# Twelve idle matrix products at the start, and position biases loaded as one run per query, in a two-layer diffusion backbone

## The chip, the cores and the metric

The kernel runs on one core of one Trainium2 chip. The metric is the device time of one execution in microseconds (us); lower is better. The engines are TensorE (PE in the profile, its weight loads PEld), VectorE (DVE), ScalarE (ACT), GpSimd (POOL) and SyncE (SP, which here only issues transfers).

## The reference: what is computed

Two layers work on 256 latent tokens (a grid of 4 rows by 64 columns, 2048 channels each) and 256 context tokens, all in float32. Both layers begin with an adaptive normalisation whose scale, shift and gate come from a conditioning vector (adaln). The first layer holds 16 heads of neighbourhood attention and 32 state-space (SSD) heads side by side, between one input projection (14,400 columns) and one output projection; the second is a gated short convolution between two projections. What matters here is the start and the attention's bias:

```python
def adaln(cond, w, b):
    m = jax.nn.silu(cond) @ w + b
    return jnp.split(m, 3, axis=-1)
...
dr_idx = rs + jnp.arange(kh) - r + NA_KH - 1
bias = rpb[:, dr_idx[None, :, None], dc_idx[:, None, :]].reshape(nh, GRID_W, kh * GRID_W)
s_lat = jnp.einsum('bqhd,bkhd->bhqk', qr, kb).astype(jnp.float32) * scale + bias.astype(jnp.float32)
s_lat = jnp.where(mask, s_lat, -jnp.inf)
```

With four grid rows each query sees all four rows of keys. Its bias in a head depends only on the difference of the rows and of the columns: for query column c, key row a and key column k it is one element of the head's table of 15 by 31, at row (a - r + 7) and column (k - c + 15). Columns outside a window of 16 are masked.

## The kernel before: tiling, stages and order

**Precision.** A product of two float32 operands is made of three passes of the fast float32r form: each operand is split into a high part (a cast, on ScalarE) and a low part (the difference, on VectorE). A weight block of 128 x 1024 is loaded into one of the `raw` buffers by SP (line 428), cast into `wH` (line 458), and its low part goes into `wL` (line 465). Only when the low part is done is the raw buffer free for the next load.

**Start.** The conditioning vector becomes `csil` and is spread into `cpad`, a zero tile of 128 x 512 with two columns filled in every 32 (lines 548 to 556, the tile Btm). SP issues the two x tiles first, four blocks of 256 KB each (`x_load`, line 618), then the ada weights of 512 KB a block, then the first weights of the input projection. The x tiles are squared, summed and scaled in place (`x_norm`, lines 636 to 650), turned by 32 transposes on TensorE (`x_pair`, line 235 by the helper `turn`) and copied out of PSUM (lines 663 and 664). The scale and shift of the first 256 channels come from eight ada blocks (`ada_gen`): four 32-column products run side by side (line 231 by the helper `mm`), ScalarE copies the sum out (line 768), two transposes turn it, and VectorE adds. Then the normalised activations are made (`hH` and `hL`, lines 798 and 804) and the projection begins. In eight rounds of j this repeats for the next 256 channels, beside products for K, V, Q and B.

**Attention bias.** After the eight rounds the table is written once to `dram_rpbs`, each head's 320 relevant elements repeated for 64 query columns (line 967). In `head_gen`, a head loads its bias tile `bt` (128 partitions: two query rows of 64 columns each, by 3 x 256) with four transfers (line 1080), one for each grid row r of queries. In `dram_rpbs` the partitions step by 319 elements in rows of 320, so that each query starts one element further to the left, and four pieces of 64 elements (one per key row, 31 apart) are fetched per partition: 256 pieces of 256 bytes per transfer. VectorE adds the column mask (line 1085), and the maximum pass adds the bias to the scores (line 1098), once with the tile's first and last third (the last is zero, for the context keys), once with its second and last. Two tiles, bias0 and bias1, alternate; the loads of a head wait until the head two before it is done.

**Order.** The code is written as generators that a planner (`Plan`) interleaves: it keeps an estimated time for each engine and for the DMA, and emits a step when its inputs are expected. The order on every engine is fixed when the program is built. SP issues its transfers strictly in order, so a load whose buffer is free stands behind every transfer issued before it. In the program's rows every SP transfer also carries one of eight completion counters in turn.

**In the state-space part** (`dt_gen`, lines 1180 to 1260) a row of 128 values is broadcast to 128 partitions from the input `in_rows` (line 1184), and lines 1201 and 1203 on VectorE use it. This stands just behind the first two heads' bias loads in SP's order.

## Time and profile before

| What | Value |
|---|---|
| Runs | 1771.32, 1767.39, 1771.30 us; median 1771.3 |
| Profiled execution | 1762.67 us |
| Its span in the profile | 1760.9 us |
| Mean granted TensorE clock | 0.999 |
| VectorE, ScalarE busy | 73%, 45% |
| DMA | 412.5 MB, mean 234 GB/s |
| DMA packets | 147,629, of which 34,304 under 512 bytes |

The profile is of one execution. A row of a timeline reads: start and length in us, engine, line of the code, operation, output and inputs by the program's names with the buffer numbers left out, shapes, number; and in brackets how long the engine was idle before and what ended that. A row of a group ends with busy time in us and the mean of one in ns. In a row of windows, the busy time of PE, PEld, DVE, ACT and POOL (with counts) is followed by the granted clock, the share of time that the DMA engines were busy, and GB/s. A float32 product that is not of the float32r form shows as two records. A releaser is inferred: where the engine named had been done long before, a transfer was meant.

### The profile page before, as it was taken

Reading aid. Unit: us, or ns where it says so; the run is one execution under the profiler, and the core shown is the slowest. Engines: PE = TensorE matmul, PEld = TensorE weight load, DVE = VectorE, ACT = ScalarE, POOL = GpSimd, SP = SyncE. Lnnn points to the kernel's source line nnn. Section 1 sums busy time; section 2 is a strip of 40 time slices with the busy share of each in tenths; the row PEclk is TensorE's granted clock in tenths of the full one; section 3 lists DMA queues with packets and bytes.
Section 4 is the critical chain, followed back from the end, with each engine's and each line's share of the span. In section 5 each row is a group of like instructions: output and inputs, shape, how many; then the busy total and the mean of one; then the engine's idle time right before and its main releaser. Section 6 shows DMA issues by size and latency. Waiting matters only on the chain.

```text
span 1760.9 us, 25272 instructions
## 1 busy us (share of the span) xinstructions
PE 1728.3 (98%) x9305; PEld 1442.4 (82%) x9305; DVE 1292.8 (73%) x2041; ACT 785.3 (45%) x1186; POOL 191.0 (11%) x300
## 2 busy tenths in 40 slices
PE   6999999999999999999999999999999999999998
PEld 4677988889888889888888898888878888888887
DVE  5566877888787987786888698876667776766555
ACT  5422335454354453353453444654435444444442
POOL 0000111013111012111012101110000000000000
PEclk9999999999999999999999999999999999999999
DMA  9987675577876677866577767787766888876774
GB/s 349 344 291 252 214 227 181 181 214 241 261 227 201 190 219 248 262 193 204 170 239 227 215 188 226 224 261 253 268 216 232 265 281 266 267 248 216 219 231 158
DMA packets 147629, 412.50 MB, mean 234 GB/s; under 512 B 34304, under 2 KB 48272, under 8 KB 147504
## 3 DMA queue, kind: packets, MB, share of 16 engines
q1 hardware_dynamic: 132112, 366.64, 64.0%
q0 software_dynamic: 15392, 44.24, 8.0%
q8 instruction: 73, 1.20, 0.3%
q14 instruction: 52, 0.43, 0.1%
HBM read 386.53 MB, written 25.59 MB: 234 GB/s over the span
## 4 chain that ended last, share of the span: by engine, by line
PE 94%; DVE 2%; DMA 1%; ACT 1%; issue 1%; SPq 0%; POOL 0%; DVEq 0%; ACTq 0%; POOLq 0%
PE bank L231 93%; PE bank L235 1%; DVE wL L465 1%; DMA raw<-in_ada_w 0%; ACT wH L458 0%; DMA half<-in_rows 0%; DVE hL L804 0%; SPq L618 0%; DMA raw<-in_sc_in 0%; DVE tmp L1283 0%; DVE h L1729 0%; DVE tmp L800 0%; ACT h L1748 0%; ACT hH L798 0%; DVE xm L664 0%
## 5 line engine op out<-in xcount | busy, mean ns | idle before, releaser
L458 ACT CAST wH<-raw 128x1024 fp32r<-128x1024 f32 (+1 forms) x440 | 459.5, 1045 | 664.0 <-PE bank L231 559.6
L465 DVE TENSOR_TENSOR wL<-raw,wH 128x1024 fp32r<-128x1024 f32 (+1 forms) x440 | 532.2, 1213 | 257.4 <-ACT wH L458 255.0
L231 PE MATMUL bank<-hH,wH 128*128 128x256 f32 (+1 forms) x1040 | 341.0, 328 | 0.9 <-ACT wH L458 0.9
L231 PE MATMUL bank<-hL,wH 128*128 128x256 f32 (+1 forms) x1040 | 337.0, 324 | 0.0
L231 PE MATMUL bank<-hH,wL 128*128 128x256 f32 (+1 forms) x1024 | 331.4, 324 | 3.1 <-DVE wL L465 3.1
L231 PE MATMUL bank<-wH,h 128*128 128x512 f32 x1024 | 316.8, 390 | 1.7 <-DVE h L1729 1.7
L231 PE MATMUL bank<-wH,hH 128*128 128x512 f32 x640 | 256.0, 400 | 4.8 <-ACT hH L798 2.6
L231 PE MATMUL bank<-wL,hH 128*128 128x512 f32 x640 | 249.9, 391 | 0.3 <-DVE wL L465 0.3
L231 PE MATMUL bank<-wH,hL 128*128 128x512 f32 x640 | 249.3, 390 | 0.1
L231 PEld LDWEIGHTS bank<-wH,h 128*128 128x128 f32 x1024 | 191.9, 188 | 43.5 <-DVE h L1729 3.0
L231 PEld LDWEIGHTS bank<-hH,wH 128*128 128x128 f32 x1040 | 197.8, 190 | 18.9 <-issue 2.0
L231 PEld LDWEIGHTS bank<-hL,wH 128*128 128x128 f32 x1040 | 197.8, 190 | 15.8
L231 PEld LDWEIGHTS bank<-hH,wL 128*128 128x128 f32 x1024 | 194.6, 190 | 19.4 <-DVE wL L465 4.1
L857 DVE SCALAR_TENSOR_TENSOR acc<-raw,csil,acc 128x512 f32<-128x512 f32 x240 | 179.1, 746 | 30.9 <-DMA raw<-in_ada_w 27.2
L231 PE MATMUL bank<-wL,h 128*128 128x512 f32 x512 | 199.4, 389 | 0.2 <-DVE wL L465 0.2
L231 PE MATMUL bank<-wH,mix 128*128 128x512 f32 x512 | 160.9, 391 | 0.0
L231 PEld LDWEIGHTS bank<-wH,hH 128*128 128x128 f32 x640 | 120.1, 188 | 36.3 <-issue 7.2
L231 PEld LDWEIGHTS bank<-wH,hL 128*128 128x128 f32 x640 | 120.1, 188 | 25.4 <-DVE hL L804 0.6
L231 PEld LDWEIGHTS bank<-wL,hH 128*128 128x128 f32 x640 | 120.1, 188 | 25.0 <-DVE wL L465 1.1
L231 PEld LDWEIGHTS bank<-wL,h 128*128 128x128 f32 x512 | 96.1, 188 | 20.6 <-DVE wL L465 0.6
L231 PEld LDWEIGHTS bank<-wH,mix 128*128 128x128 f32 x512 | 96.1, 188 | 20.4 <-issue 0.5
L231 PE MATMUL bank<-wL,mix 128*128 128x512 f32 x256 | 99.7, 390 | 0.0
(276 smaller groups left out, 1856.5 us busy)
## 6 DMA issues: line engine op xcount, KB each, us to landing
raw<-in_w_in SPq DMA_DIRECT2D x209, 512.0 KB
raw<-in_ada_w SPq DMA_DIRECT2D x163, 512.0 KB
raw<-in_sc_in SPq DMA_DIRECT2D x128, 512.0 KB
raw<-in_w_out SPq DMA_DIRECT2D x64, 512.0 KB
raw<-in_sc_out SPq DMA_DIRECT2D x32, 512.0 KB
dram_ptd<-tmp POOLq DMA_DIRECT2D x32, 256.0 KB, 4.9
D<-dram_ptd POOLq DMA_DIRECT2D x64, 128.0 KB, 5.6
tmp<-dram_csr SPq DMA_DIRECT2D x32, 256.0 KB
```

Of the source, the lines that this page charges most:

```text
L231: E(T.matmul(o, l, r, start=start, stop=stop, skip_group_check=True))
L235: E(T.transpose(o, i, ident if k == 128 else ident[:k, :k]))
L458: E(S.copy(H, v))
L465: E(V.tensor_tensor(out=Lo, in0=v, in1=H.bitcast(F32), op=ALU.subtract))
L857: E(V.scalar_tensor_tensor(out=acc, in0=v[:, j], scalar=csil[:, 2 * k + j:2 * k + j + 1], in1=acc, op0=ALU.mult, op1=ALU.add))
```

## The change

**Idle products.** Right after the loads of the two x tiles are issued, 12 products of 128 x 256 are written for TensorE, into PSUM bank 7, whose content nobody reads before it is written again. Eight take both operands from `cpad`; four take the moving operand from the four blocks of the second x tile, so they wait for its loads. They go around the planner, which knows nothing of them.

**Bias.** The four pieces of a query lie 31 elements apart and are 64 long, so they overlap, and two query rows differ by 31 more. Each head now loads one contiguous run of 219 elements (876 bytes) per partition with two transfers, one per half of the partitions, to the end of the tile's first two thirds (`runs`, from column 293). The mask addition reads the overlapping pieces out of the run and writes them apart, from the front, into the same tile. The two halves of the tile have changed places, so line 1098 takes them the other way round. The planner is told to count each of the two transfers as two of the old kind.

```diff
+            twice = n == 4 * 64 * 219
             self.t[e] = s + (1200 if e == "POOL" else 450)
+            if twice:
+                n = 65536
+                self.dma = max(self.dma, s + 1000) + n / self.RATE
+                s += 450
+                self.t[e] += 450
...
     x_load(0)
     x_load(1)
+    flat = cpad.rearrange("p a b -> p (a b)")
+    for k in range(12):
+        T.matmul(free_b[7][:, :256], flat[:, :128], flat[:, :256] if k < 8 else XS[k - 4][:, :256], start=True, stop=True,
+                 skip_group_check=True)
     issue()
...
         yield W_("SP")
-        for r in range(4):
-            E(DMA.dma_start(bt[64 * (r % 2):64 * (r % 2) + 64, r // 2, :].rearrange("p (a b) -> p a b", a=4),
-                            bass.AP(tensor=b0.tensor, offset=b0.offset + hd * 64 * 320 + (7 - r) * 31 - 61,
-                                    ap=[[319, 64], [31, 4], [1, 64]])))
+        runs = bt[:, 0:2, :].rearrange("p q c -> p (q c)")[:, 293:]
+        for e in range(2):
+            E(DMA.dma_start(runs[64 * e:64 * e + 64],
+                            bass.AP(tensor=b0.tensor, offset=b0.offset + hd * 64 * 320 + 94 - 31 * e, ap=[[319, 64], [1, 219]])))
         yield W_("DVE", bt)
-        bv = bt[:, 0:2, :].rearrange("p q (r c) -> p (q r) c", c=64)
-        E(V.tensor_tensor(out=bv, in0=bv, in1=mask.unsqueeze(1).to_broadcast([128, 8, 64]), op=ALU.add))
+        E(V.tensor_tensor(out=bt[:, 0:2, :].rearrange("p q (r c) -> p q r c", c=64),
+                          in0=bass.AP(tensor=runs.tensor, offset=runs.offset, ap=[list(runs.ap[0]), [62, 2], [31, 4], [1, 64]]),
+                          in1=mask.unsqueeze(1).unsqueeze(1).to_broadcast([128, 2, 4, 64]), op=ALU.add))
...
-            E(V.tensor_tensor_reduce(out=two(sp), in0=two(ps), in1=bt[:, 1:3, :] if qt else bt[:, 0::2, :], scale=1.0,
+            E(V.tensor_tensor_reduce(out=two(sp), in0=two(ps), in1=bt[:, 0::2, :] if qt else bt[:, 1:3, :], scale=1.0,
```

The new lines push the rest of the code down by 6 to 11 lines, so line 231 of before is line 237 of the changed kernel, line 428 is 434 and line 1080 is 1091. The rows of the program below carry their own kernel's numbers.

TensorE at the very start of the program, before (raw are ada blocks, xs the x tiles, const the identity for the transposes):

```order
L2000 UNCONDITIONAL_BRANCH
L231 MATMUL bank_127<-raw_135,cpad 32x256 x4
L231 MATMUL bank_127<-raw_136,cpad 32x256 x4
L235 MATMUL bank_128<-const,xs_169 128x128
L235 MATMUL bank_128<-const,xs_177 128x128
```

And in the changed kernel:

```order
L2011 UNCONDITIONAL_BRANCH
L631 MATMUL bank_134<-cpad 128x256 x8
L631 MATMUL bank_134<-xs_177,cpad 128x256
L631 MATMUL bank_134<-xs_179,cpad 128x256
L631 MATMUL bank_134<-xs_181,cpad 128x256
L631 MATMUL bank_134<-xs_183,cpad 128x256
L237 MATMUL bank_127<-raw_135,cpad 32x256 x4
L237 MATMUL bank_127<-raw_136,cpad 32x256 x4
L241 MATMUL bank_128<-const,xs_169 128x128
L241 MATMUL bank_128<-const,xs_177 128x128
```

The twelve stand ahead of everything else; xs_177 to xs_183 are the second x tile. All rows behind them are the same as before, in the same order, and so are all rows of VectorE, ScalarE and GpSimd.

SP around the first two heads' bias loads, before (in_w_in and in_ada_w are weights):

```order
L428 DMA raw_135<-in_w_in 128x1024
L428 DMA raw_137<-in_w_in 128x1024
L1080 DMA bias_217<-dram_rpbs 64x4x64 x4
L1080 DMA bias_218<-dram_rpbs 64x4x64 x4
L428 DMA raw_139<-in_w_in 128x1024
L428 DMA raw_135<-in_w_in 128x1024
L428 DMA raw_136<-in_ada_w 128x1024
L428 DMA raw_138<-in_ada_w 128x1024
L428 DMA raw_137<-in_w_in 128x1024
L1184 DMA half_125<-in_rows 128x128
```

And in the changed kernel:

```order
L434 DMA raw_135<-in_w_in 128x1024
L434 DMA raw_137<-in_w_in 128x1024
L1091 DMA bias_229<-dram_rpbs 64x219 x2
L1091 DMA bias_230<-dram_rpbs 64x219 x2
L434 DMA raw_139<-in_w_in 128x1024
L434 DMA raw_135<-in_w_in 128x1024
L434 DMA raw_136<-in_ada_w 128x1024
L434 DMA raw_138<-in_ada_w 128x1024
L434 DMA raw_137<-in_w_in 128x1024
L1195 DMA half_125<-in_rows 128x128
```

Eight transfers have become four at the same place, and nothing around them has moved. The other fourteen heads differ in the same way, with two transfers where there were four.

## Prediction

> **What bounds the kernel now.** I read the page's head and its chain first, then the waits of TensorE, then the two stretches in which TensorE stands still beside something that the change touches. The page's first line, the TensorE line, and the chain by engine:

> ```profile
> span 1760.9 us, 25272 instructions
> PE 1728.3 (98%) x9305; PEld 1442.4 (82%) x9305; DVE 1292.8 (73%) x2041; ACT 785.3 (45%) x1186; POOL 191.0 (11%) x300
> ...
> PE 94%; DVE 2%; DMA 1%; ACT 1%; issue 1%; SPq 0%; POOL 0%; DVEq 0%; ACTq 0%; POOLq 0%
> ```

> TensorE is busy for 98% of the span and is 94% of the chain that ended last. Whatever is taken off the other engines is worth only what it takes out of the 32.6 us (1760.9 less 1728.3) in which TensorE is idle. The waits of TensorE, longest first (us in total, times, longest):

> ```profile
> PE bank L231 <- DVE rx L606: 13.1, 1, 13.1
> PE bank L231 <- DVE wL L465: 3.6, 5, 2.3
> ```

> The first is the start of the program, the second holds one single stall of 2.3 us. The change touches just these two.

> The profiled execution took 1762.67 us: its span and 1.8 us around it. The median of the three runs shown is 1771.3 (1767.39 to 1771.32). I work out a difference on the profiled execution and take it from the median. What a measurement of this kernel can tell from no change is about 0.3%, 5.3 us.

> **The idle products: 12 matmuls, ahead of all others.** The chain of waits at the start (start us, us, what), with one later row for comparison:

> ```profile
> 5.92 8.35 DMA raw<-in_ada_w
> 14.31 1.08 PE bank L231 x8
> 15.39 4.78 PE bank L235 x32
> 20.17 1.04 PE bank L231 x16
> ...
> 21.66 0.44 PE bank L235 x2
> 22.10 1.91 PE bank L231 x32
> ...
> 26.12 8.94 PE bank L231 x36
> ...
> 226.90 0.44 PE bank L235 x4
> ```

> From the landing of the second ada block at 14.31 the chain runs through TensorE without a break until 21.2. The same work is slower there than later: eight ada records take 1.08 us, then sixteen take 1.04; a transpose takes 4.78/32 = 0.149 us, later 0.44/4 = 0.11. The groups by shape, in four narrow windows (13 to 13.8, 16.3 to 16.8, 18.3 to 18.8 us, and the whole span for the last), give the mean of one:

> ```profile
> L231 PE MATMUL bank<-raw,cpad 128*32 128x256 f32 x8 | 1.1, 631 | 13.1 <-DVE rx L606 13.1
> ...
> L235 PE MATMUL bank<-const,xs 128*128 128x128 f32 x4 | 1.1, 421 | 0.0
> ...
> L235 PE MATMUL bank<-const,xs 128*128 128x128 f32 x7 | 0.9, 273 | 0.0
> ...
> L231 PE MATMUL bank<-tmp,Btmt 128*128 128x256 f32 x32 | 8.2, 379 | 0.0
> ```

> The array starts slow after 13.1 us of idling and gets fast between 16.8 and 18.3, some 4.4 us after its first product, although the granted clock of the windows below reads 1.00. Had it been fast at 14.31, the chain would lose 1.08 - 0.52 = 0.56 us on the ada records and 4.78 - 32 x 0.11 = 1.26 on the transposes: 1.82 in all, and 21.2 becomes 19.4.

> [...]

> Are the idle products early enough? Rows of VectorE and ScalarE (the last write of cpad, the squares of the x blocks, their scaling in place), and TensorE around its later stall:

> ```profile
> 3.42 0.17 DVE L556 COPY cpad<-csil 128x16 f32<-128x16 f32 x1
> ...
> 8.28 0.69 DVE L638 CUSTOM_DVE_ANT_0 tmp<-xs 128x512 f32<-128x512 f32 x1 [1.91 <-DMA xs<-in_x]
> ...
> 11.74 0.69 DVE L638 CUSTOM_DVE_ANT_0 tmp<-xs 128x512 f32<-128x512 f32 x1
> ...
> 13.72 1.33 ACT L648 ACTIVATE xs<-xs,rx 128x512 f32<-128x512 f32 x2 [1.04 <-POOL rx L607]
> ...
> 244.01 0.39 PE L231 MATMUL bank<-hH,wL 128*128 128x256 f32 x1 [2.33 <-DVE wL L465]
> 244.24 0.28 PE L231 MATMUL bank<-hH,wH 128*128 128x256 f32 x1
> 244.36 0.28 PE L231 MATMUL bank<-hL,wH 128*128 128x256 f32 x1
> ```

> Products of this shape are the Btmt group: two records each, 8.2/16 = 0.51 us when fast, I take 1.02 when slow. Eight can start at 3.6; 4.4 us slow is 4.3 of them, the other 3.7 take 1.9, so they end at 9.9. The last four need the blocks of the second x tile, which land after 8.28 (VectorE still waited for the first tile) and by 11.74 (no wait). So they end between 12.0 and 12.3, before the first ada block at 13.1. The idle time until then, 1.1 us or less, should not cost the speed: after 2.33 us of idling the array was fast at once (0.12 us from one product to the next at 244.24).

> The change adds two waits. On TensorE the four products wait for the second x tile, and the ada products and transposes are queued behind them. The scaling in place of that tile at 13.72 waits for the four, and behind it on ScalarE and VectorE are the evacuations of the transposes. By the count above both are over in time; where they overran, the cost is in the rivals. The later users of bank 7 follow on the same engine.

> What is late next is the second group of ada blocks, since TensorE comes 1.8 us sooner. At the DMA rate of 10 to 13 us, the first of two rows of the windows,

> ```profile
> 10.00:13.00 3.00, 0.00 (x0) 0.00 (x0) 2.44 (x8) 2.56 (x6) 0.09 (x1) 1.00 1.04 423
> ...
> 40.00:50.00 10.00, 9.73 (x108) 7.15 (x108) 5.94 (x20) 6.25 (x17) 0.01 (x1) 1.00 0.98 377
> ```

> (the last three columns are granted clock, DMA share and GB/s) a block of 0.524 MB takes 1.24 us, as the first two (13.1, 14.31) do; the eighth is in at 14.31 + 6 x 1.24 = 21.75. TensorE would want it at 19.4 + 0.9 (evacuation and two transposes, 21.21 to 22.10 now) + 24 x 0.06 = 21.7. It just fits, 0.1 lost. The first weight block is then in at 23.0, half of it cast by some 23.6 (a whole cast takes 1.04, ScalarE row below), and the products of 26.12 start at about 24.4. I take **1.6 us**. The lower bound is 0.5, if a block lands 1.1 later than by rate here or in the next rounds, since the queues stay full (share 0.98 from 40 to 50); the upper is 1.82. I pass the 1.6 on whole, because the list of TensorE's waits names no transfer after the start.

> **The bias transfers: 64 become 32.** The first eight are the ones beside a stall. SP's queue, what VectorE and ScalarE then wait for, and the DMA in two windows (share, GB/s at the end):

> ```profile
> 225.08 7.26 SPq L1080 DMA_DIRECT2D bias<-dram_rpbs  x8
> 232.44 1.02 SPq L428 DMA_DIRECT2D raw<-in_w_in  x2
> 233.55 0.86 SPq L428 DMA_DIRECT2D raw<-in_ada_w  x2
> 234.79 0.33 SPq L428 DMA_DIRECT2D raw<-in_w_in  x1
> 235.17 0.51 SPq L1184 DMA_DIRECT2D half<-in_rows  x1
> ...
> 226.89 1.22 DVE L465 TENSOR_TENSOR wL<-raw,wH 128x1024 fp32r<-128x1024 f32 x1 [1.56 <-ACT wH L458]
> ...
> 229.40 1.22 DVE L465 TENSOR_TENSOR wL<-raw,wH 128x1024 fp32r<-128x1024 f32 x1
> ...
> 242.40 0.43 DVE L1203 TENSOR_TENSOR half<-half,half 128x256 f32<-128x256 f32 x1 [6.09 <-DMA half<-in_rows]
> 242.74 2.35 DVE L465 TENSOR_TENSOR wL<-raw,wH 128x1024 fp32r<-128x1024 f32 x2
> ...
> 242.23 1.04 ACT L458 CAST wH<-raw 128x1024 fp32r<-128x1024 f32 x1 [2.70 <-DMA raw<-in_w_in]
> ...
> 230.00:235.00 5.00, 5.00 (x35) 4.59 (x34) 4.25 (x6) 1.79 (x3) 0.00 (x0) 1.00 0.86 169
> 235.00:240.00 5.00, 5.00 (x44) 5.00 (x44) 1.31 (x3) 2.47 (x3) 0.00 (x0) 1.00 1.01 410
> ```

> Eight issues hold SP's queue for 7.26 us. Two raw buffers are free at 228.1 and 230.6 (the ends of the L465 rows), but their loads stand behind the bias and go out at 232.44, five within 2.7 us. The transfer of in_rows stands behind all five and lands at 242.3; VectorE waits 6.09 us for it, the low half of a weight block waits behind VectorE, and TensorE waits 2.33 for that. After the change four issues take 4 x 0.33 to 4 x 0.9 (a weight load's; 7.26/8), 1.3 to 3.6 us: SP is free by 226.4 to 228.7, and the loads go out as buffers come free. Two or three blocks have then landed by 235.2, and in_rows lands 2.5 to 3.7 us sooner (two or three times 0.524 MB at 410 GB/s is 1.28 each), at 238.6 to 239.8. VectorE's L1203 and one L465 take 1.6 more: 241.4 at the latest, where TensorE needs it at 241.7. The stall goes: **2.3 us**, at least 0.5 (should in_rows come only 0.5 sooner), at most 2.33. No lost speed is behind it, since the array was fast after it. The other 14 heads' transfers lie beside a busy TensorE; a faster SP gains nothing there.

> The mask addition and the maximum keep their place and count:

> ```profile
> L1085 DVE TENSOR_TENSOR bias<-bias,const x16: 650/684/704, 234.7 to 1143.1; 128x512 f32<-128x512 f32 x16
> ```

> The addition reads overlapping runs in place of one even row, the same 512 elements a partition; I count no change. The swap of the halves and the planner's doubled cost change no order, so nothing else moves.

> **The sum**: 1.6 + 2.3 = 3.9 us. The span becomes 1757.0, the profiled execution 1758.8; from the median, 1771.3 - 3.9 = 1767.4.

> **Rivals.**
> The idle products do nothing: they end slow, or the array slows again in the gap or in the transposes (the 32 transposes then stay at 4.78 us). The change of speed within the transposes speaks against it. The start then gives 0 to 0.56; with the 2.3 of the stall the time is 1768.4 to 1769.0. [...]

> The stall stays: in_rows or the cast of 242.23 is late for the blocks still ahead of it, and a later weight block stalls instead. The wait of ScalarE at 242.23 speaks for it, but its load also stood in the burst. Only the start gives: 1769.7.

> More comes: in runs of 1767 to 1771 other loads may be late that the profiled run, 5 to 9 us shorter, does not show, and fewer transfers help there. Over 5.3 us, 1765 or less.

> Slower: the addition of the mask pays for its overlapping rows. Were each twice as long, 16 x 0.684 = 10.9 us are added on VectorE, at places where, with 73% busy, low halves of weights queue behind it. If all reached TensorE, the net is +7.0: 1778.3. It turns the sum from 3.9/16 = 0.24 us an addition on. For it speaks only that no row shows such reads; against it, that the row's length goes with its elements. A smaller mishap on the same side, slow idle products until 3.6 + 12 x 1.02 = 15.9, holds the ada records by 1.6 us and eats the start's gain.

> **How the numbers follow.** Forecast with both terms 0.56; products of no use 0.14; stall stays 0.12; more comes 0.12; slower 0.06. The predicted time is the first's, 1767.4. The unknown costs make the forecast 1.0 to 4.2 us, 1770.3 to 1767.1; with runs that themselves differ by 3.9 us from one to the next, 1763.2 holds such a gain measured on a low run, and 1771.2 one measured on a high one. Faster by over 0.3% takes "more comes" and about a sixth of the forecast's runs, 0.22; slower 0.05 of the last rival; within 0.3% the rest, 0.73.

> **What would show it.** Right: records of the first ada blocks near 385 ns instead of 631, the first products on wH near 24.4, SP's bias issues half as many, no wait of over 1 us for in_rows, TensorE without the 2.33 us stall near 240. Wrong: 421-ns transposes again, TensorE waiting for raw before 24, a stall of 2 us elsewhere between 230 and 260, mask additions over 0.9 us. A gain over 5.3 us would say that I missed a wait.

## The result, and the profile after

| | before | after |
|---|---|---|
| Median of 22 runs each, alternating | 1770.28 us | 1762.72 us |
| Lowest to highest | 1764.53 to 1773.35 | 1760.24 to 1766.83 |
| Profiled execution | 1762.67 us | 1766.83 us |

The ratio after to before is 0.9964, with a 95% interval of 0.9956 to 0.9972: a gain of 6.4 us (5.0 to 7.8). That is the ratio of the means; the two medians lie 7.6 us apart. Forecast were 3.9 us. The median is 4.7 us below the predicted time and 0.5 us below the low end of the range; the gain is a little over the 0.3% that I had called the limit of what can be told, to which I had given a chance of 0.22.

A warning comes first. The execution of before that was profiled was faster than all 22 timed ones beside it, and the profiled one of after was the slowest of its 22. The page's first line of after:

```profile
span 1764.9 us, 25268 instructions
```

Against 1760.9 before, the two spans alone say that the change costs 4.0 us. So the profiles are read here place by place, and the time is taken from the many runs.

**The start.** TensorE's timeline of after (start, length, line, operation; in brackets the idle time before and what ended it):

```profile
3.70 6.13 PE L631 MATMUL bank<-cpad 128*128 128x256 f32 x16 [3.70 <-DVE cpad L562]
11.21 2.63 PE L631 MATMUL bank<-xs,cpad 128*128 128x256 f32 x8 [1.38 <-DMA xs<-in_x]
...
15.69 0.64 PE L237 MATMUL bank<-raw,cpad 128*32 128x256 f32 x8 [0.65 <-DMA raw<-in_ada_w]
16.26 3.73 PE L241 MATMUL bank<-const,xs 128*128 128x128 f32 x32
...
25.93 0.74 PE L237 MATMUL bank<-wH,hH 128*128 128x512 f32 x2 [1.22 <-ACT hH L808]
```

The eight ada records take 0.64 us in place of 1.08, the 32 transposes 3.73 in place of 4.78. From the second ada group to the first product on wH it is 10.24 us (25.93 less 15.69) against 11.81 (26.12 less 14.31): 1.57 us saved. That is against one profile of before. In the six profiles with nothing ahead of the first ada block (of the kernels below, too) the stretch takes 11.30 to 12.27 us, in the five with all twelve products 10.24 to 10.32: the saving is 1.0 to 2.0 us. In this execution only 0.2 us of it is seen (25.93 against 26.12), since the second ada block happened to land 1.4 us later than in the profile of before; between the profiles shown here that landing wanders from 13.75 to 15.69.

The trace's own clock records begin at 17.70 us in the profile of before, in the midst of the transposes, and at 8.61 us in this one, during the idle products. Ahead of the first record the windows print 1.00, so that column, which the prediction quotes for the start, says nothing there.

**The stall near 241.** Rows of SP, VectorE and TensorE, after:

```profile
225.00 2.42 SPq L1091 DMA_DIRECT2D bias<-dram_rpbs  x4
228.12 3.96 SPq L434 DMA_DIRECT2D raw<-in_w_in  x2
232.41 1.90 SPq L434 DMA_DIRECT2D raw<-in_ada_w  x2
...
235.50 0.42 SPq L1195 DMA_DIRECT2D half<-in_rows  x1
...
240.94 0.43 DVE L1214 TENSOR_TENSOR half<-half,half 128x256 f32<-128x256 f32 x1 [4.31 <-DMA half<-in_rows]
...
242.56 0.39 PE L237 MATMUL bank<-hH,wL 128*128 128x256 f32 x1 [0.95 <-DVE wL L471]
242.78 0.28 PE L237 MATMUL bank<-hH,wH 128*128 128x256 f32 x1
```

The bias holds SP for 2.42 us in place of 7.26 and the weight loads go out as their buffers come free, not in one burst. in_rows is issued no earlier than before (235.50), but from 232.4 us to then three weight loads are issued ahead of it, where it were five: VectorE has it at 240.94, 1.5 us sooner, and TensorE's wait shrinks from 2.33 to 0.95 us.

The bias tile's own rows (shortest, median, longest in ns):

```profile
L1091 SPq DMA_DIRECT2D bias<-dram_rpbs x32: 450/587/2484, 225.0 to 1140.5; - x32
L1094 DVE TENSOR_TENSOR bias<-bias,const x16: 649/685/703, 235.0 to 1147.1; 128x512 f32<-128x512 f32 x16
```

Half as many issues, and the mask addition, 684 ns before, costs the same on overlapping rows.

**A stall that before's profile does not have.** VectorE and TensorE of after around 303, and the windows there (granted clock, DMA share and GB/s are the last three columns):

```profile
296.98 1.54 DVE L867 SCALAR_TENSOR_TENSOR acc<-raw,csil,acc 128x512 f32<-128x512 f32 x2 [5.67 <-DMA raw<-in_ada_w]
298.44 1.22 DVE L471 TENSOR_TENSOR wL<-raw,wH 128x1024 fp32r<-128x1024 f32 x1
299.57 5.31 DVE L1294 SCALAR_TENSOR_TENSOR tmp<-bank,cwh,tmp 128x508 f32<-128x508 f32 x7
304.80 1.22 DVE L471 TENSOR_TENSOR wL<-raw,wH 128x1024 fp32r<-128x1024 f32 x1
...
306.07 0.58 PE L237 MATMUL bank<-hH,wL 128*128 128x256 f32 x1 [2.57 <-DVE wL L471]
306.45 0.42 PE L237 MATMUL bank<-hH,wH 128*128 128x256 f32 x1
```

```profile
240.00:250.00 10.00, 9.05 (x57) 8.05 (x56) 8.85 (x13) 3.46 (x6) 2.31 (x4) 1.00 0.59 185
300.00:310.00 10.00, 7.43 (x52) 7.23 (x51) 9.79 (x14) 4.48 (x6) 0.00 (x0) 0.83 0.49 159
```

VectorE waits 5.67 us for an ada block, and what stands behind it in VectorE's order ends at 306.0, 2.57 us after TensorE ran out. Then the products take 0.42 us where they took 0.28 at 242.78, and the mean granted clock of the slice is 0.83. A narrow window shows what that is, half speed for 3.4 us:

```profile
305.57:308.98 3.41, 2.91 (x13) 2.91 (x14) 3.41 (x5) 1.65 (x3) 0.00 (x0) 0.50 0.48 154
```

That is 1.7 us of clock. A part of it falls into the waiting, since TensorE starts again only at 306.07: from there sixty products take 8.57 us, where the same sixty take 7.30 at full speed (idle products alone, below), so 1.3 us are lost. This stall, and the fall of the clock behind it, are what the experiments had to place.

### The profile page after: what moved, and what is told of

It is laid out like the page before. It is cut to its first block, busy times and chain, and to the rows that moved or that the text cites. A ratio compares the mean times of both kernels' runs of the same rounds, so it can differ in the third digit from the quotient of the medians.

```text
span 1764.9 us, 25268 instructions
## 1 busy us (share of the span) xinstructions
PE 1736.8 (98%) x9329; PEld 1448.2 (82%) x9329; DVE 1292.7 (73%) x2041; ACT 785.5 (45%) x1186; POOL 191.0 (11%) x300
## 4 chain that ended last, share of the span: by engine, by line
PE 90%; DVE 4%; DMA 3%; issue 1%; ACT 1%; SPq 0%; POOL 0%; DVEq 0%; ACTq 0%; POOLq 0%
PE bank L237 89%; DVE wL L471 2%; PE bank L241 1%; DMA raw<-in_ada_w 1%; DMA raw<-in_w_in 1%; ACT wH L464 0%; DVE tmp L1294 0%; DMA kqD_K<-dram_kqd 0%; DVE acc L867 0%; DMA half<-in_rows 0%; DVE hL L814 0%; SPq L624 0%; DVE h L1740 0%; DVE tmp L1034 0%; DVE tmp L810 0%
## 5 line engine op out<-in xcount | busy, mean ns | idle before, releaser
L237 PEld LDWEIGHTS bank<-hL,wH 128*128 128x128 f32 x1040 | 198.4, 191 | 15.7
```

Of the source, the lines that this page charges most:

```text
L237: E(T.matmul(o, l, r, start=start, stop=stop, skip_group_check=True))
```

## The experiments

Ten kernels, in three groups; those of a group ran on one chip, beside runs of the kernel before. The first four take the change apart and repeat it. Theory A is the forecast's sum, 1.6 and 2.3 us; in B the bias transfers hold loads at many places; in C the start is worth 4 us or more.

### The two parts alone, and both ends again

Bias alone leaves out the twelve products:

```diff
-    for k in range(12):
-        T.matmul(free_b[7][:, :256], flat[:, :128], flat[:, :256] if k < 8 else XS[k - 4][:, :256], start=True, stop=True,
-                 skip_group_check=True)
```

> The whole change was measured at 0.9964 of before, some 6.4 us, where 3.9 were forecast. Theory A (the forecast's sum, each term as it was worked out): bias runs alone give 2.3 us, a ratio of 0.9987. Theory B (the bias transfers held up loads at many places, most of which one profiled execution of before does not show): 5 to 6.5 us, 0.9963 to 0.9972, nearly the whole change. Theory C (the start is worth more than its 1.6 us): 2 us or less, 0.9989 or more.

Idle products alone is the kernel before with those lines added:

> Theory A: idle products alone give 1.6 us, a ratio of 0.9991. Theory B: 0 to 1 us, 0.9994 to 1.0, since in the profile of the changed kernel the products on wH began only 0.2 us sooner than before (25.93 in place of 26.12), held by the second ada block, which landed at 15.7 in place of 14.3. Theory C: 4 us or more, 0.9977 or less.

The changed kernel and the kernel before, unedited:

> The changed kernel once more, for a second profile and time beside its parts. All theories: 0.9956 to 0.9972 of before. If the parts add up, this ratio less one is the sum of those of the two parts. In the profile, theory A expects no stall of TensorE over 1 us between 30 and 700 us; theory B expects stalls whose places differ from those of the first profile (303 us 2.57, 240 us 0.95, 723 us 1.25), because they hang on when single loads land.

> The kernel before against itself: ratio 1.000 within 0.001. Its profile is a second one of the same program. Theory A expects the stall of 2.33 us near 241 again and no other over 1 us between 100 and 1300 us. Theory B expects further stalls of 1 to 3 us at places that the first profile did not show, since the first execution was at 1762.7 faster than all 22 timed ones (1764.5 to 1773.4).

| Kernel | Median, us | Ratio to before (1768.85) | Interval |
|---|---|---|---|
| bias alone | 1765.95 | 0.9984 | 0.9970 to 0.9998 |
| idle products alone | 1767.94 | 0.9989 | 0.9974 to 1.0004 |
| both (the change) | 1763.56 | 0.9973 | 0.9959 to 0.9987 |
| before again | 1769.14 | 1.0002 | 0.9989 to 1.0015 |

The parts give 2.8 and 1.9 us, the whole 4.8: they add up, and neither carries the gain alone as theories B and C had it. The intervals are wide, though: that of the bias (0.4 to 5.3 us) just reaches theory B's 5 us, and that of the idle products (a loss of 0.7 to a gain of 4.6) reaches theory C's 4 us and holds no gain at all. The second measure of the change (2.3 to 7.3 us) and the first (5.0 to 7.8) overlap. Both parts come out a little above their terms of the forecast, 2.3 and 1.6 us, each well within its interval.

The traces show both terms. With the idle products alone, TensorE's start again saves 1.5 us (24.05 less 13.75 is 10.30):

```profile
13.75 0.64 PE L231 MATMUL bank<-raw,cpad 128*32 128x256 f32 x8 [0.60 <-DMA raw<-in_ada_w]
14.32 3.71 PE L235 MATMUL bank<-const,xs 128*128 128x128 f32 x32
...
24.05 0.73 PE L231 MATMUL bank<-wH,hH 128*128 128x512 f32 x2 [1.23 <-ACT hH L802]
...
242.22 0.58 PE L231 MATMUL bank<-hH,wL 128*128 128x256 f32 x1 [2.48 <-DVE wL L465]
242.60 0.41 PE L231 MATMUL bank<-hH,wH 128*128 128x256 f32 x1
```

Its last two rows are the stall near 241, which stays without the new bias loads. It is 0.15 us longer than in the first profile of before, and now the products behind it are slow. In the second profile of before the stall is 2.73 us, and the window (granted clock third from the end) shows the same:

```profile
240.00:250.00 10.00, 7.27 (x50) 7.07 (x49) 5.61 (x8) 3.21 (x6) 0.13 (x1) 0.83 0.60 220
```

So the stall costs its own length and, in these two of three profiles, a fall of the clock behind it: the next sixty products take 12.61 and 12.68 us, where they took 11.37 in the first profile of before, 1.2 and 1.3 us more. With the bias alone TensorE does not stop near 241 at all:

```profile
240.00:250.00 10.00, 10.00 (x65) 9.07 (x65) 9.15 (x14) 3.76 (x7) 2.31 (x4) 1.00 0.61 197
```

### Does the bias gain go through in_rows, and is it issues or pieces?

The load of in_rows in the kernel before is moved up, into a tile that is free there; the bias keeps its four transfers a head:

```diff
+    csl = st([128, 2, 64], "csl")
+    rwd = csl.rearrange("p a b -> p (a b)")
+    rwl = DMA.dma_start(rwd, rows[0].partition_broadcast(128))
     rpbs = drt([16, 64, 320], "rpbs")
...
-        E(DMA.dma_start(rw[:, :128], rows[0].partition_broadcast(128)))
+        E(rwl)
```

> The kernel before with its eight bias issues as they were, but the load of in_rows is issued some 20 us earlier (ahead of the write of the bias table), into a tile that is free until then. Theory P (the bias term of the forecast goes through in_rows alone): the stall of 2.3 to 2.7 us near 241 goes although SP still issues eight bias transfers in 7.3 us; with it the fall of the granted clock that followed in two of three profiles; ratio to before 0.9975 to 0.9988 (2.1 to 4.4 us), like the bias change alone (0.9984). Theory Q (the weight loads that stand behind the bias are late in themselves, in_rows is only the last to be seen): a stall of 1.5 us or more stays near 241, now at a cast that waits for its raw block, and the ratio is 0.9993 to 1.0.

Measured: 1763.87 us against 1768.96, ratio 0.9980 (0.9968 to 0.9992), 3.5 us. Theory P. SP and VectorE, and the window:

```profile
226.61 8.27 SPq L1083 DMA_DIRECT2D bias<-dram_rpbs  x8
...
238.28 0.42 DVE L1206 TENSOR_TENSOR half<-half,csl 128x256 f32<-128x256 f32 x1
```

```profile
240.00:250.00 10.00, 10.00 (x69) 9.28 (x69) 7.76 (x10) 4.51 (x7) 2.31 (x4) 1.00 0.85 319
```

SP is held as long as ever, the weight loads go out in the same late burst, and TensorE is busy for all of the 10 us: only in_rows had mattered. One load moved up gives what the new bias loads give (3.5 and 2.8 us, with intervals that overlap).

The changed kernel with the same early load:

> The changed kernel with the same early load of in_rows. Theory P: the 0.7 to 0.95 us that TensorE still stands near 241 goes, nothing else of the bias part is left: 0.5 to 1 us faster than the changed kernel (0.9964 and 0.9973 so far), ratio to before 0.996 to 0.9970. Theory Q: it comes out like the changed kernel, and TensorE still waits there for a weight block. The stall of 2.6 to 2.9 us near 303, seen in both profiles of the changed kernel and in none of the bias change alone, is a matter of this run too: if it comes from TensorE being early it is there again, if it was chance it may be missing.

Measured: 1763.57, ratio 0.9970 (0.9958 to 0.9982), no wait left near 241. The 0.5 to 1 us expected on top of the change is too small to tell from 0.9973 and 0.9964. Theory P's mechanism holds; its number stays open.

The changed kernel with twice as many transfers, each of half the partitions:

```diff
-        for e in range(2):
-            E(DMA.dma_start(runs[64 * e:64 * e + 64],
+        for e in range(4):
+            E(DMA.dma_start(runs[32 * e:32 * e + 32],
```

> The changed kernel with its runs of 219 elements fetched by four transfers of 32 partitions a head instead of two of 64: as many bytes and pieces as in the changed kernel, as many transfers as before. If the number of issues sets what SP is held (0.6 us each in the changed kernel), the first eight hold it some 4.8 us instead of 2.4, in_rows lands 1 to 2 us later and TensorE stands 1.5 to 2.7 us near 241: ratio to before 0.9976 to 0.9988. If the time of an issue goes by its pieces, the eight take 2.4 to 3 us, the stall stays at 0.7 to 1 us and the ratio is that of the changed kernel, 0.9964 to 0.9973.

Measured: 1767.56, ratio 0.9994 (0.9982 to 1.0007). By this ratio the whole bias gain is gone, although each query's run is still one piece. SP's own waits between 224 and 234 us (total, times, longest), in before first and then in this kernel:

```profile
SPq L1080 <- DMA raw<-in_w_in: 2.1, 1, 2.1
```

```profile
SPq L1087 <- DMA raw<-in_w_in: 3.9, 2, 2.4
```

This kernel's issues (ns), and the timeline and window of its stall:

```profile
L1087 SPq DMA_DIRECT2D bias<-dram_rpbs x64: 302/420/1967, 225.0 to 1146.9; - x64
```

```profile
242.66 0.43 DVE L1211 TENSOR_TENSOR half<-half,half 128x256 f32<-128x256 f32 x1 [6.10 <-DMA half<-in_rows]
...
244.28 0.58 PE L233 MATMUL bank<-hH,wL 128*128 128x256 f32 x1 [2.69 <-DVE wL L467]
244.66 0.41 PE L233 MATMUL bank<-hH,wH 128*128 128x256 f32 x1
```

```profile
240.00:250.00 10.00, 7.32 (x43) 6.86 (x42) 7.27 (x9) 3.25 (x6) 1.81 (x4) 0.83 0.51 175
```

Neither of the two expectations had this right; the first had the length of the stall (1.5 to 2.7 us), but neither what holds SP nor the time. An issue does get cheaper with fewer pieces (420 ns against 615), but the eight hold SP for 7.30 us all the same, because the seventh and the eighth wait 3.9 us for a weight block to land. In the trace of before all 841 transfers of SP carry eight completion counters in turn, so the eighth bias transfer has the counter of the weight load issued just before the bias, at 224.70: that counter has the last of the block at 231.75, and the eighth goes out at 231.77, after 2.1 us of waiting. Here the eighth waits 2.4 us, in before with in_rows early 3.1. So what held SP in the first profile of before was 8 x 0.62 us of issuing and a wait of 2.1 us for the counter. Four transfers stop short of that (no bias transfer of the changed kernel waits for a block between 224 and 234 us); eight do not, not even eight of half the size.

The comparison suggests a price of the stall: against the changed kernel it is 0.9994 - 0.9973 = 0.21%, 3.7 us, for a stall that is 1.7 to 2.0 us longer (2.69 against 0.95 and 0.74) and the 1.5 us that the slow phase behind it costs here (sixty products in 12.84 us). The two ratios are of different groups and their intervals overlap a little. Nor need all of it come from this place: this kernel's profile has two more falls of the clock, at 725 and 1132 us, that no other profile has, and the mean granted clock of its timed runs is 0.9972, against 0.9985 in the changed kernel. Whether the other heads' transfers have to do with these two is open.

### Is it the idling that makes the clock fall?

Products of no use are put into the waits of the kernel before. The four near 241 add zeros (the bias tile's last third) to the bank that the waiting product adds to:

```diff
+        if calls[0] == 33:
+            f_ = cpad.rearrange("p a b -> p (a b)")
+            for _ in range(2):
+                T.matmul(o[:, :256], f_[:, :128], f_[:, :256], start=True, stop=True, skip_group_check=True)
+        if calls[0] == 1131:
+            for _ in range(4):
+                T.matmul(o, ident, bias[0][:, 2, :], start=False, stop=False, skip_group_check=True)
```

> The kernel before with products of no use in two places where TensorE waits: two on cpad ahead of the first product on wH (1.2 us of waiting), four that add zeros ahead of the product that waits 2.3 to 2.7 us near 241. They fit into the waiting, so the waits themselves stay. Theory R (the runs of before lose 1.7 us each time that the granted clock falls to 0.83 for 10 us after a wait of about 2.4 us or more, and the change saves some of these): no slice of the profile between 20 and 260 us is below 0.97, the mean clock of the timed runs rises from 0.998 by about 0.0005, and the time falls by 0.5 to 2 us (ratio 0.9989 to 0.9997). Without R (the clock falls for other reasons): ratio 0.9997 to 1.0005, and falls of the clock at 20 to 30 or 240 to 250 as before.

Measured: 1768.38, ratio 1.0002 (0.9990 to 1.0014): no gain. TensorE's timeline:

```profile
240.61 1.89 PE L240 MATMUL bank<-bias,const 128*128 128x256 f32 x8
244.68 0.58 PE L241 MATMUL bank<-hH,wL 128*128 128x256 f32 x1 [2.18 <-DVE wL L475]
245.06 0.42 PE L241 MATMUL bank<-hH,wH 128*128 128x256 f32 x1
```

The four filled 1.89 us, but in this execution the gap was 4.1 us long, and the 2.18 left of it were enough: the products behind are slow. It tells nothing against theory R and nothing for it. So six were put there, and the two at the start left out:

> The kernel before with six products that add zeros (0.47 us each) ahead of the product that waits near 241; nothing at the start. Four of them left a wait of 2.18 us behind them in e7, and the clock fell to 0.83 all the same. Theory R (it is the idle time of 1.8 us or more that makes the clock fall): with 2.8 us filled, 0 to 1.3 us of idling are left, the granted clock is 1.00 at 240 to 250, and the products behind it come 0.12 us apart; the product that waits still starts when its low half is ready, or up to 0.5 us later; ratio to before 0.9989 to 1.0. If the clock falls for another reason, it reads 0.83 there again, products come 0.21 us apart, ratio 1.0 or above.

Measured: 1769.34, ratio 0.9997 (0.9985 to 1.0009). The same place:

```profile
242.25 2.75 PE L236 MATMUL bank<-bias,const 128*128 128x256 f32 x12
245.21 0.39 PE L237 MATMUL bank<-hH,wL 128*128 128x256 f32 x1 [0.21 <-DVE wL L471]
245.43 0.28 PE L237 MATMUL bank<-hH,wH 128*128 128x256 f32 x1
```

```profile
240.00:250.00 10.00, 9.79 (x64) 8.77 (x63) 6.37 (x8) 4.16 (x7) 0.88 (x2) 1.00 0.64 218
```

The critical path is as late as before, only the array was kept at work, and the clock stays at 1.00. In the profile theory R holds at this place, but it is one profile, and in one of before the clock had stayed up after 2.33 us of waiting. In the time the 1 us or so does not rise above the interval. That the change saves some falls is seen in the mean granted clock of the timed runs: 0.9980 for the kernel before in the 70 runs of the first two groups, 0.9985 for the changed kernel in its 34; 0.0005 of 1765 us is 0.9 us.

### Are the four products on the x tile needed?

The changed kernel with the first eight alone:

```diff
-    for k in range(12):
+    for k in range(8):
```

> The changed kernel with the eight idle products on cpad alone; the four that wait for the second x tile are left out, so TensorE idles from about 8 to 9.8 us until the first ada block at 13.3 to 14.4, some 4 to 6 us in place of 0.6. If the array must be kept at work until the ada block comes, it is slow again: the first eight ada records near 631 ns, the 32 transposes 4.6 to 4.8 us, from the second ada group to the first product on wH 11.6 to 11.8 us, and the ratio is that of the bias change alone, near 0.9984. If eight early products were enough, the records are near 385 ns, the transposes 3.7, the stretch 10.25, and the ratio that of the changed kernel, 0.9964 to 0.9973.

Measured: 1764.83, ratio 0.9975 (0.9964 to 0.9987), which cannot tell the two expectations apart. The trace can. TensorE's timeline and one window:

```profile
3.60 5.26 PE L631 MATMUL bank<-cpad 128*128 128x256 f32 x16 [3.60 <-DVE cpad L562]
13.11 0.68 PE L237 MATMUL bank<-raw,cpad 128*32 128x256 f32 x8 [4.25 <-DMA raw<-in_ada_w]
14.35 1.08 PE L237 MATMUL bank<-raw,cpad 128*32 128x256 f32 x8 [0.56 <-DMA raw<-in_ada_w]
15.36 6.15 PE L241 MATMUL bank<-const,xs 128*128 128x128 f32 x32
...
27.46 0.73 PE L237 MATMUL bank<-wH,hH 128*128 128x512 f32 x2 [1.22 <-ACT hH L807]
```

```profile
10.00:20.00 10.00, 6.33 (x38) 5.00 (x39) 4.35 (x13) 4.74 (x12) 0.55 (x1) 0.68 1.03 420
```

After 4.25 us of idling the first ada group is still fast (0.68), the second is slow (1.08), and the clock is at half from 13.58 to 20.41 us:

```profile
13.58:20.41 6.83, 6.27 (x36) 5.25 (x33) 2.66 (x7) 3.20 (x7) 0.06 (x1) 0.50 1.03 420
```

The transposes take 6.15 us, longer than with no idle products at all: from the second group on it is 13.1 us against 11.8 before and 10.2 with all twelve. In this execution eight products are worse than none. How often it goes so is open. A loss of 2.9 us against the change would be a ratio of 0.9980 to 0.9989, and the interval holds the lower part of that; the mean granted clock of the timed runs, 0.9970 against 0.9985 in the changed kernel, points to such a loss in many of them, the median time does not.

### The stall near 303

It came up in nearly every later profile, so it can be laid against the landing of its ada block. In order of the time from SP's issue to the start of VectorE's waiting instruction:

| Profile | Landing, us | TensorE idle near 303, us | Clock behind it |
|---|---|---|---|
| bias alone | 5.8 | 0 | 1.00 |
| before again | 5.9 | 0 | 1.00 |
| idle products alone | 6.3 | 0.7 | 1.00 |
| before | 6.4 | 0 | 1.00 |
| four transfers | 7.5 | 1.1 | 1.00 |
| fills (on before) | 7.6 | 1.8 | 0.98, then 0.85 |
| change, in_rows early | 7.6 | 1.9 | 0.83 |
| after | 8.1 | 2.6 | 0.83 |
| before, in_rows early | 8.3 | 2.5 | 0.83 |
| change again | 8.8 | 2.9 | 0.83 |

The clock is the mean of a 10-us slice. The last kernels (eight products; six zeros on before) had it too, 2.45 and 2.13 us. It goes with the landing time of one block, and it does not need the change: three kernels with neither of its parts have it (before with in_rows early, and with either of the two fills). That the idle products make it likelier is not ruled out, though: all six profiles with them at the start have it (0.7 to 2.9 us), and neither profile of the unedited kernel before nor that of the bias alone does. Each of these loads goes out within 0.9 us of four transfers that GpSimd issues. Why one block takes 5.8 us and another 8.8 there was not settled; no kernel was made for it.

## Why the prediction fell short

- **The start: right.** 1.6 us were forecast, the traces show 1.0 to 2.0; against the profile that the sum was made on it is 1.5 to 1.6. In the profile of after they ended at 13.8, not at 12.0 to 12.3, because the x tile landed later; the ada block did too. The step "the idle time until then, 1.1 us or less, should not cost the speed" held (0.55 and 0.65 us). The rival in which the idle products do nothing, with the transposes at 4.78 us and at most 0.56 us to gain, is refuted: the transposes take 3.73, 1.05 us less.
- **The bias, its path: right.** Moving in_rows alone gives as much, and TensorE then never stops there. The doubled mask addition of the rival that ends slower is refuted by 685 ns against 684. "The stall stays" is refuted as well.
- **The bias, how it works: wrong.** I priced an issue at 7.26/8 = 0.9 us and took in_rows to be late by the number of bytes ahead of it. The issues cost 0.62; the rest was one wait of 2.1 us for a completion counter. in_rows came 1.5 us sooner, not 2.5 to 3.7, VectorE still waited 4.31 us for it, where no wait of over 1 us had been named as the sign of being right, and 0.7 to 0.95 us of the stall stayed, where I had taken off all 2.33.
- **The step that failed:** "No lost speed is behind it, since the array was fast after it." That was one execution. In three other profiles with the stall (2.48, 2.69 and 2.73 us) the clock falls to half for 3.4 us, which costs the products behind it 1.2 to 1.5 us. So the term is about 1.4 to 2.0 us of waiting and 1.2 to 1.5 us of slow products in three of four, 2.3 to 3.1 us, where I put 2.3 with 2.33 as its upper bound: the waiting was put too high and the clock at nothing. With the start's 1.6 that makes 3.9 to 4.7 us, inside the second measure (2.3 to 7.3) and below the first (5.0 to 7.8). So the missing term makes up for what stayed of the stall and at most 0.8 us more. The 1.7 to 2.5 us that are left to 6.4 have no cause shown here; the two measures of the change themselves differ by 1.6.
- **The base.** Of the 4.7 us between the predicted time and the median, 1.0 is the base: the sum was taken from 1771.3, the median of three runs, and that of 22 is 1770.28. And I made the sum on an execution faster than all 22 timed beside it. Just there the clock had not fallen behind the stall; the second profile of before shows the missing term. "More comes" was the rival nearest to the outcome, but other late loads were not its cause: of those only in_rows mattered near 241, and the one near 303 is there without the change too.

## What to carry to other kernels

A stall on TensorE cost more than its length where the clock fell behind it (1.2 to 1.5 us on top of 2.48 to 2.73), and whether it did is read from the spacing of the products after it, in more than one profile. A load that a critical instruction needs belongs ahead of a batch of transfers: moving one 64 KB load up was worth as much as halving 64 transfers (3.5 and 2.8 us, with intervals that overlap). Products of no use at a start should reach up to the moment when the real work starts: in the one profile where they ended 4.25 us early, the start was worse than with none (13.1 us against 11.8 from the second ada group to the first product on wH).
